# A hybrid encoder block on one core: query latent with its rows outermost, both halves of x in one 256-column block, norm scales per token

## The chip, the cores and the metric

One core of a Trainium2 chip runs one layer of a streaming encoder for 256 tokens. The metric is the device time of one execution in microseconds (us). PE is the matrix engine (TensorE), with a weight load (PEld) ahead of each matmul; DVE is VectorE, ACT is ScalarE, POOL is GpSimd, SP issues the transfers of weights.

## The reference, cut to what matters

```
u = rms_norm(x, norm_pre_mix)                      # x: 256 tokens x 2048
q_sb, k_sb, v_sb, q_lat, kv_lat, k_r, gates = split(u @ w_in)   # widths 1024, 1024, 1024, 768, 512, 64, 4096
y_sb  = stick_breaking_attention(q_sb, k_sb, v_sb) @ w_o_sb
q     = rms_norm(q_lat, q_norm) @ w_uq             # nope and rope parts of 8 heads
kv    = rms_norm(kv_lat, kv_norm) @ w_ukv
y_mla = mla_attention(q, rope(k_r), kv) @ w_o_mla
h     = x + rms_norm((gate_sb * y_sb + gate_mla * y_mla) @ w_out)
out   = h + rms_norm(swiglu(rms_norm(h)) @ w_down)
```

Everything is float32. `rms_norm(x, g)` divides each token by the root of its mean square and multiplies each column by g.

## The kernel before, in words

Every product of a weight w and an activation x is made of three fp32r products: both are split into a high part (an ACT copy to fp32r) and a low part (a DVE subtraction), and hi*hi + hi*lo + lo*hi is summed in PSUM. Weights stream from HBM in units of 128 x 1024 (512 KB) over SP's queue: `unit` (L88) issues the transfer into `raw`, ACT makes `hi` (L101), DVE makes `lo` (L102). There are four buffers of each.

The first stages put features on the output partitions and the 256 tokens on the columns. `pair` (L154) makes 256 features: for each row block k of 128 rows and each half j of 128 features it issues one matmul of 512 columns (the high weights times both halves of x, side by side, L164) and one of 256 columns (the low weights times the high half of x, L166). I call these two matmuls, for one k and one j, a step. The result lies in PSUM as two halves of 256 columns, which `fold` (L171) adds: an ACT copy of one half (L173), a DVE addition (L174), and where a norm scale applies a DVE multiplication by a row of 256 per-token scales (L176).

The order of the work: three pairs of the query latent (`lat_q`, 6 x 128 features), two of the key/value latent (`lat_kv`), the rope key (`kr`, the same two matmuls at L364 and L365), four pairs of `q_sb`, then from the latents `qn` (four pairs, K = 6 blocks), `qr` (two), `kn` (four, K = 4), then `vm`, `k_sb`, `v_sb` and the gates, and after them the output products and the SwiGLU. That is 536 steps: 96 for lat_q, 64 for lat_kv, 16 for kr, 128 each for q_sb and k_sb, 48 for qn, 24 for qr, 32 for kn. The later stages (`token` L178, `two_products` L612) use matmuls of 512 columns only.

The first pair also loads x: `load_first` (L212) puts the transfers of x (L113) between those of the weights, in small pieces for the first four row blocks, and ACT and DVE split x (L115, L116). So all 2 MB of x pass during the first pair, that is, during its four units.

The weights of the norms are folded into x or the latents; the per-token scales are applied after the products. `x_stats` (L227) sums squares of x (ACT squares, POOL additions), `x_scale` (L239) turns the sum over features into a row of scales (`row_sums`, L130, one fp32 matmul of 256 columns with ones) and into a column of scales (`col_sums`, L135), each through `rsqrt` (L120: ACT Sqrt and five DVE operations). `lat_scale` (L408) does the same for both latents. `angles` (L275) is a chain of DVE operations for the rope.

These side jobs are hung on unit numbers: `at_unit(u, f)` emits f behind the matmuls of unit u, and behind that unit's splits on ACT and DVE. The lat_q units are 0 to 11, lat_kv 12 to 19, kr 20 and 21, q_sb 22 to 37. Within these rules the framework's planner orders each engine's instructions; each engine then runs them in that order.

Of the kernel before, what the change touches and what calls it, by code (L numbers as in the profile page):

```python
# [53 lines left out]
def block_kernel(ctx: ExitStack, tc: tile.TileContext, a: dict, out: bass.AP):  # L54
# [14 lines left out]
    def at_bank(name):  # L69
        return pat.tile([P, 512], F32, tag="at", name=name)  # L70
# [17 lines left out]
    def unit(stream, cols_n, cuts=1, first=None):  # L88
        off = streams.get(stream, 0)
        streams[stream] = off + P * cols_n  # L90
        src = a[stream][off:off + P * cols_n].rearrange("(p c) -> p c", p=P)
        raw = wp.tile([P, 1024], F32, tag="raw", name=f"raw_{stream}_{off}", bufs=4)
        hi = wp.tile([P, 1024], F32R, tag="hi", name=f"hi_{stream}_{off}", bufs=4)
        lo = wp.tile([P, 1024], F32R, tag="lo", name=f"lo_{stream}_{off}", bufs=4)
        w = cols_n // cuts
        for c in range(cuts):
            cs = slice(c * w, c * w + w)
            if first:
                first(c)
# [30 lines left out]
    def row_sums(acc, name):  # L130
        ps = at_bank(f"{name}_row")
        TE.matmul(ps[:, :T], lhsT=ones, rhs=acc, start=True, stop=True)
        return ps[:, :T]
# [20 lines left out]
    def pair(name, stream, K, per, rhs, first=None):  # L154
        ps = mm_pair(f"{name}_ps")
        for u in range(K // per):
            cuts = (4 if u == 0 else 2) if first else 1
            hi, lo = unit(stream, per * 2 * P, cuts, first and (lambda c: first(u, c)))
            for i in range(per):
                k = u * per + i  # L160
                for j in range(2):
                    o = (i * 2 + j) * P
                    r = rhs(k)
                    TE.matmul(ps[:, j, :], lhsT=hi[:, o:o + P], rhs=r, start=k == 0, stop=False,  # L164
                              skip_group_check=True)
                    mm = TE.matmul(ps[:, j, 0:T], lhsT=lo[:, o:o + P], rhs=r[:, 0], start=False, stop=k == K - 1,  # L166
                                   skip_group_check=True)
            unit_done(mm)
        return ps

    def fold(ps, row, out_t):  # L171
        tb = tmp.tile([P, 2, T], F32, tag="t2", name="tb", bufs=6)
        S.activation(tb, ps[:, :, T:], AF.Copy)  # L173
        V.tensor_tensor(out_t, ps[:, :, 0:T], tb, op=ALU.add)  # L174
        if row is not None:
            V.tensor_tensor(out_t, out_t, row[:, None, :].to_broadcast([P, 2, T]), op=ALU.mult)  # L176
# [62 lines left out]
    def x_scale():  # L239
        acc = acc_x[0]  # L240
        v = slot("vx")[:, 0]
        V.tensor_scalar(v, row_sums(acc, "x"), 1.0 / D, EPS, op0=ALU.mult, op1=ALU.add)
        rsqrt(r0, v)
        vc = const.tile([P, 2], F32, tag="vxc", name="vxc")
        V.tensor_scalar(vc, col_sums(acc, "x"), 1.0 / D, EPS, op0=ALU.mult, op1=ALU.add)
        rsqrt(r0c, vc)
        V.tensor_tensor(r0_sq[:, 0], r0, r0, op=ALU.mult)
        V.tensor_tensor(r0c_sq, r0c, r0c, op=ALU.mult)
        V.tensor_scalar_mul(r0q, r0, SB_SCALE)
# [75 lines left out]
    lat = {}  # L325
    for nm, n in (("q", 6), ("kv", 4)):
        acc = slot(f"acc_{nm}")[:, 0]
        g = cols[f"{nm}_norm"]
        for p in range(n // 2):
            first = nm == "q" and p == 0  # L330
            ps = pair(f"lat_{nm}{p}", "w_lat", KD, 4, xk, load_first if first else None)
            s = tmp.tile([P, 2, T], F32, tag="t2", name="s", bufs=6)
            fold(ps, None, s)
# [14 lines left out]
        lat[nm] = acc  # L348

# [10 lines left out]
    for u in range(2):  # L360
        hi, lo = unit("w_kr", 1024)
        for i in range(8):
            k = u * 8 + i
            TE.matmul(kps, lhsT=hi[:, i * P:i * P + P], rhs=xs[:, k], start=k == 0, stop=False, skip_group_check=True)  # L364
            mm = TE.matmul(kps[:, 0:T], lhsT=lo[:, i * P:i * P + P], rhs=xs[:, k, 0], start=False, stop=k == KD - 1,  # L365
                           skip_group_check=True)
        unit_done(mm)
    kraw = slot("kraw")[:, 0]

    def take_k():  # L370
        kb = slot("kb")[:, 0]
        S.activation(kb, kps[:, T:], AF.Copy)
        V.tensor_tensor(kraw, kps[:, 0:T], kb, op=ALU.add)
        V.tensor_tensor(kraw, kraw, r0, op=ALU.mult)

    at_unit(count[0] + 1, take_k)
# [3 lines left out]
    def proj_q(p):  # L380
        ps = pair(f"q_sb{p}", "w_q", KD, 4, xk)
        t = slot(f"q_sb{p}")
        fold(ps, r0q, t)
        qsb.append(t)

    def proj_k(p):
        ps = pair(f"k_sb{p}", "w_k", KD, 4, xk)
        t = slot(f"k_sb{p}")
        fold(ps, r0, t)
        ksb.append(t)  # L390
# [12 lines left out]
    at_unit(26, rope_k)  # L403
# [446 lines left out]
def _lay_out(x, positions, norm_pre_mix, w_in, b_gate, q_norm, w_uq, kv_norm, w_ukv, w_o_sb, w_o_mla, w_out,  # L850
# [21 lines left out]
        "w_lat": _feature_units(w, 3072 + ar(1280), 4),  # L872
# [36 lines left out]
```

## Time and profile before

| what | us |
|---|---|
| median of 3 runs | 1394.98 (1394.79 to 1395.91) |
| the profiled execution | 1395.33 |
| its span, first to last instruction | 1393.6 |
| PE busy | 1373.6 |
| DVE busy | 804.1 |
| ACT busy | 681.1 |

Read the engines' busy shares first, then what PE waited for, then the stretch in which it waited.

### The profile page before, as it was taken

Reading aid. Unit: us, or ns where it says so; the run is one execution under the profiler, and the core shown is the slowest. Engines: PE = TensorE matmul, PEld = TensorE weight load, DVE = VectorE, ACT = ScalarE, POOL = GpSimd, SP = SyncE. Lnnn points to the kernel's source line nnn. Section 1 sums busy time; section 2 is a strip of 40 time slices with the busy share of each in tenths; the row PEclk is TensorE's granted clock in tenths of the full one; section 3 lists DMA queues with packets and bytes.
Section 4 is the critical chain, followed back from the end, with each engine's and each line's share of the span. In section 5 each row is a group of like instructions: output and inputs, shape, how many; then the busy total and the mean of one; then the engine's idle time right before and its main releaser. Section 6 shows DMA issues by size and latency. Waiting matters only on the chain.

```text
span 1393.6 us, 16788 instructions
## 1 busy us (share of the span) xinstructions
PE 1373.6 (99%) x6400; PEld 1141.1 (82%) x6400; DVE 804.1 (58%) x927; ACT 681.1 (49%) x816; POOL 59.2 (4%) x89
## 2 busy tenths in 40 slices
PE   7999999999999999999999999999999999999997
PEld 6888888888888888887888888888888888888886
DVE  7997966555555566557555545555455555444444
ACT  7564454466548443445644444444444454434343
POOL 3210000000002100000000000000000001000001
PEclk9999999999999999999999999999999999999999
DMA  7565655455567766664766666665656666666663
GB/s 239 186 207 164 199 167 166 153 182 183 172 209 250 219 184 190 185 196 121 218 190 184 192 186 193 184 191 185 195 185 192 184 207 205 192 196 195 195 188 116
DMA packets 74977, 262.88 MB, mean 189 GB/s; under 512 B 8592, under 2 KB 9744, under 8 KB 74768
## 3 DMA queue, kind: packets, MB, share of 16 engines
q1 hardware_dynamic: 72720, 254.86, 58.8%
q0 software_dynamic: 1744, 6.29, 1.4%
q8 instruction: 50, 0.82, 0.2%
q10 hardware_dynamic: 432, 0.66, 0.1%
q14 instruction: 31, 0.25, 0.0%
HBM read 259.68 MB, written 2.10 MB: 188 GB/s over the span
## 4 chain that ended last, share of the span: by engine, by line
PE 94%; DVE 3%; DMA 1%; ACT 1%; issue 1%; SPq 0%; POOL 0%; DVEq 0%; ACTq 0%
PE gu_ps L629 11%; PE gu_ps L631 11%; PE gu_ps L630 11%; PE wd_ps L200 6%; PE wd_ps L202 6%; PE wd_ps L201 6%; PE gate_ps L202 4%; PE gate_ps L200 4%; PE gate_ps L201 4%; PE k_sb_ps L164 2%; PE q_sb_ps L164 2%; PE wout_ps L200 2%; PE wout_ps L202 2%; PE wo_ps L631 2%; PE wo_ps L630 2%; PE wo_ps L629 2%
## 5 line engine op out<-in xcount | busy, mean ns | idle before, releaser
L773 DVE SCALAR_TENSOR_TENSOR lo_w_gu<-raw_w_gu,packed,hi_w_gu 128x1024 fp32r<-128x1024 f32 x172 | 221.0, 1285 | 213.3 <-ACT hi_w_gu L772 211.6
L772 ACT ACTIVATE hi_w_gu<-raw_w_gu,packed 128x1024 fp32r<-128x1024 f32 x172 | 198.0, 1152 | 230.4 <-PE gu_ps L630 226.4
L629 PE MATMUL gu_ps<-hi_w_gu,hs 128*128 128x512 f32 x704 | 276.6, 393 | 0.9 <-ACT hi_w_gu L766 0.9
L631 PE MATMUL gu_ps<-lo_w_gu,hs 128*128 128x512 f32 x704 | 275.1, 391 | 0.7 <-DVE lo_w_gu L767 0.7
L630 PE MATMUL gu_ps<-hi_w_gu,hs 128*128 128x512 f32 x704 | 273.5, 389 | 0.0
L102 DVE TENSOR_TENSOR lo_w_down<-raw_w_down,hi_w_down 128x1024 fp32r<-128x1024 f32 x88 | 109.2, 1242 | 120.4 <-ACT hi_w_down L101 120.1
L101 ACT ACTIVATE hi_w_down<-raw_w_down 128x1024 fp32r<-128x1024 f32 x88 | 93.3, 1061 | 135.6 <-PE wd_ps L201 127.4
L629 PEld LDWEIGHTS gu_ps<-hi_w_gu,hs 128*128 128x128 f32 x704 | 132.2, 188 | 31.2 <-ACT hi_w_gu L766 2.3
L631 PEld LDWEIGHTS gu_ps<-lo_w_gu,hs 128*128 128x128 f32 x704 | 132.1, 188 | 28.7 <-DVE lo_w_gu L767 1.4
L630 PEld LDWEIGHTS gu_ps<-hi_w_gu,hs 128*128 128x128 f32 x704 | 132.2, 188 | 27.1
L102 DVE TENSOR_TENSOR lo_w_gate<-raw_w_gate,hi_w_gate 128x1024 fp32r<-128x1024 f32 x64 | 78.7, 1234 | 70.1 <-ACT hi_w_gate L101 63.8
L200 PE MATMUL gate_ps<-hi_w_gate,xs 128*128 128x512 f32 x256 | 100.6, 393 | 0.0
L202 PE MATMUL gate_ps<-lo_w_gate,xs 128*128 128x512 f32 x256 | 99.7, 390 | 0.0
L201 PE MATMUL gate_ps<-hi_w_gate,xs 128*128 128x512 f32 x256 | 99.6, 389 | 0.0
L101 ACT ACTIVATE hi_w_gate<-raw_w_gate 128x1024 fp32r<-128x1024 f32 x64 | 67.4, 1055 | 62.0 <-PE gate_ps L201 53.7
L102 DVE TENSOR_TENSOR lo_w_out<-raw_w_out,hi_w_out 128x1024 fp32r<-128x1024 f32 x32 | 39.2, 1226 | 38.8 <-ACT hi_w_out L101 38.6
L101 ACT ACTIVATE hi_w_o<-raw_w_o 128x1024 fp32r<-128x1024 f32 x32 | 34.0, 1061 | 51.7 <-PE wo_ps L630 45.2
L102 DVE TENSOR_TENSOR lo_w_o<-raw_w_o,hi_w_o 128x1024 fp32r<-128x1024 f32 x32 | 39.2, 1225 | 32.0 <-ACT hi_w_o L101 31.4
L101 ACT ACTIVATE hi_w_out<-raw_w_out 128x1024 fp32r<-128x1024 f32 x32 | 34.0, 1061 | 47.2 <-PE wout_ps L201 36.3
L202 PEld LDWEIGHTS gate_ps<-lo_w_gate,xs 128*128 128x128 f32 x256 | 48.0, 188 | 10.1
L201 PEld LDWEIGHTS gate_ps<-hi_w_gate,xs 128*128 128x128 f32 x256 | 48.1, 188 | 9.7
L200 PEld LDWEIGHTS gate_ps<-hi_w_gate,xs 128*128 128x128 f32 x256 | 48.1, 188 | 9.6
(447 smaller groups left out, 2557.0 us busy)
## 6 DMA issues: line engine op xcount, KB each, us to landing
raw_w_gu<-in_w_gu SPq DMA_DIRECT2D x176, 512.0 KB, 3.6
raw_w_down<-in_w_down SPq DMA_DIRECT2D x88, 512.0 KB, 3.5
raw_w_gate<-in_w_gate SPq DMA_DIRECT2D x64, 512.0 KB, 3.6
raw_w_o<-in_w_o SPq DMA_DIRECT2D x32, 512.0 KB, 3.8
raw_w_out<-in_w_out SPq DMA_DIRECT2D x32, 512.0 KB, 3.5
raw_w_lat<-in_w_lat SPq DMA_DIRECT2D x16, 512.0 KB, 4.8
raw_w_q<-in_w_q SPq DMA_DIRECT2D x16, 512.0 KB, 4.0
raw_w_k<-in_w_k SPq DMA_DIRECT2D x16, 512.0 KB, 3.8
```

Of the source, the lines that this page charges most:

```text
L101: split_ins[0] = S.activation(hi[:, cs], raw[:, cs], AF.Copy)
L102: split_ins[1] = V.tensor_tensor(lo[:, cs], raw[:, cs], hi[:, cs].bitcast(F32), op=ALU.subtract)
L164: TE.matmul(ps[:, j, :], lhsT=hi[:, o:o + P], rhs=r, start=k == 0, stop=False, skip_group_check=True)
L200: TE.matmul(ps[t], lhsT=l[0][:, ts], rhs=hi[:, cs], start=k == 0, stop=False)
L201: TE.matmul(ps[t], lhsT=l[1][:, ts], rhs=hi[:, cs], start=False, stop=False)
L202: mm = TE.matmul(ps[t], lhsT=l[0][:, ts], rhs=lo[:, cs], start=False, stop=k == K - 1)
L629: TE.matmul(ps[t][:, j], lhsT=x[0][:, ts], rhs=hi[j], start=k == 0, stop=False)
L630: TE.matmul(ps[t][:, j], lhsT=x[1][:, ts], rhs=hi[j], start=False, stop=False)
L631: mm = TE.matmul(ps[t][:, j], lhsT=x[0][:, ts], rhs=lo[j], start=False, stop=k == K - 1)
L772: split_ins[0] = S.activation(hi, raw, AF.Copy, scale=g)
L773: split_ins[1] = V.scalar_tensor_tensor(lo, raw, g, hi.bitcast(F32), op0=ALU.mult, op1=ALU.subtract)
```

## The change

The query latent is no longer three pairs one after the other. `first_products` runs over the 16 row blocks k outermost: one unit is now 128 rows x 768 features (384 KB), and for each k all six feature blocks are multiplied, into three PSUM banks that stay open together; the last two row blocks go bank by bank, so that the banks end one after the other. `load_x` is called as the row blocks come. A step is now `block`: three matmuls of 256 columns into one 256-column block (hi times x hi, hi times x lo, lo times x hi), in `pair`, in `first_products` and for `kr`. A pair then needs one bank, and there are no halves to add: `scaled` is one DVE multiplication that reads PSUM, and the latents are read by ACT and DVE straight from PSUM. The norm scales are worked out for [128, 2] columns only (`col_sums`, `rsqrt` on two columns); `spread` makes rows of them: for each 128 tokens a DVE multiplication of a block of ones by the column, a matmul with the identity (fp32, 128 columns), and an ACT copy with a factor. The side jobs hang on other unit numbers (q latent 0 to 15, kv latent 16 to 23, kr 24 and 25, q_sb 26 to 41). The host lays out the q part of `w_lat` in row order.

```diff
-    def row_sums(acc, name):
-        ps = at_bank(f"{name}_row")
-        TE.matmul(ps[:, :T], lhsT=ones, rhs=acc, start=True, stop=True)
+    def spread(col, name, *rows):
+        ps = at_bank(f"{name}_row")
+        b = tmp.tile([P, 2, P], F32, tag="t2", name="b", bufs=6)
+        for t in range(2):
+            V.tensor_scalar_mul(b[:, t], ones, col[:, t:t + 1])
+            TE.matmul(ps[:, t * P:t * P + P], lhsT=b[:, t], rhs=ident, start=t == 0, stop=True, skip_group_check=True)
+        for row, factor in rows:
+            S.activation(row, ps[:, :T], AF.Copy, scale=factor)
...
+    def block(ps, hi, lo, x, start, stop):
+        TE.matmul(ps, lhsT=hi, rhs=x[:, 0], start=start, stop=False, skip_group_check=True)
+        TE.matmul(ps, lhsT=hi, rhs=x[:, 1], start=False, stop=False, skip_group_check=True)
+        return TE.matmul(ps, lhsT=lo, rhs=x[:, 0], start=False, stop=stop, skip_group_check=True)
...
-                    TE.matmul(ps[:, j, :], lhsT=hi[:, o:o + P], rhs=r, start=k == 0, stop=False,
-                              skip_group_check=True)
-                    mm = TE.matmul(ps[:, j, 0:T], lhsT=lo[:, o:o + P], rhs=r[:, 0], start=False, stop=k == K - 1,
-                                   skip_group_check=True)
+                    mm = block(ps[:, j], hi[:, o:o + P], lo[:, o:o + P], rhs(k), k == 0 and j == 0, k == K - 1)
...
-    def fold(ps, row, out_t):
-        tb = tmp.tile([P, 2, T], F32, tag="t2", name="tb", bufs=6)
-        S.activation(tb, ps[:, :, T:], AF.Copy)
-        V.tensor_tensor(out_t, ps[:, :, 0:T], tb, op=ALU.add)
-        if row is not None:
-            V.tensor_tensor(out_t, out_t, row[:, None, :].to_broadcast([P, 2, T]), op=ALU.mult)
+    def scaled(ps, row, out_t):
+        V.tensor_tensor(out_t, ps, row[:, None, :].to_broadcast([P, 2, T]), op=ALU.mult)
...
-    for u in range(3, 12):
+    for u in [*range(2, 17, 2), 17]:
         at_unit(u, lambda: next(stat_steps, None))
     at_unit(8, constants)
-    at_unit(18, x_scale)
-    for u in [*range(5, 14), 16]:
+    at_unit(22, x_scale)
+    at_unit(24, lambda: spread(r0c, "r0", (r0, 1.0), (r0q, SB_SCALE)))
+    for u in (17, 19, 21, 23, 25, 27, 29, 31, 33, 35):
         at_unit(u, lambda: next(trig_steps, None))
...
+    def first_products():
+        both = mm_pair("lat_q_ps")
+        ps = [x.rearrange("p (j t) -> p j t", j=2) for x in (both[:, 0], both[:, 1], at_bank("lat_q2_ps"))]
+        order = [(k, p) for k in range(KD - 2) for p in range(3)]
+        order += [(k, p) for p in range(3) for k in range(KD - 2, KD)]
+        w = {}
+        for k, p in order:
+            if k not in w:
+                if k < 4:
+                    load_x(k, 1)
+                elif k % 2 == 0:
+                    load_x(k, 2)
+                w[k] = unit("w_lat", 768, 3 if k < 2 else 1)
+            hi, lo = w[k]
+            for j in range(2):
+                o = (2 * p + j) * P
+                mm = block(ps[p][:, j], hi[:, o:o + P], lo[:, o:o + P], xk(k), k == 0 and j == 0, k == KD - 1)
+            if p == 2:
+                unit_done(mm)
+            if k == KD - 1:
+                yield ps[p]
...
-    at_unit(count[0] + 1, take_k)
+        V.tensor_tensor(kraw, kps[:, 0:T], r0, op=ALU.mult)
+    at_unit(count[0] + 2, take_k)
...
-    at_unit(25, lambda: lat_scale(rq, row_sums, lat["q"], r0, r0_sq[:, 0], 768, "q", MLA_SCALE))
-    at_unit(29, lambda: lat_scale(rkv, row_sums, lat["kv"], r0, r0_sq[:, 0], 512, "kv"))
-    at_unit(32, lambda: lat_scale(rkvc, col_sums, lat["kv"], r0c, r0c_sq, 512, "kvc"))
+    at_unit(27, lambda: lat_scale(rqc, "q", 768))
+    at_unit(28, lambda: lat_scale(rkvc, "kv", 512))
+    at_unit(30, lambda: spread(rqc, "rq", (rq, MLA_SCALE)))
+    at_unit(31, lambda: spread(rkvc, "rkv", (rkv, 1.0)))
```

## Rows read from the trace of the kernel before

**Rows 1.** The page's first part: busy time, share of the span, instructions.

```profile
PE 1373.6 (99%) x6400; PEld 1141.1 (82%) x6400; DVE 804.1 (58%) x927; ACT 681.1 (49%) x816; POOL 59.2 (4%) x89
```

**Rows 2.** Waits of PE, whole span: total us, times, longest us.

```profile
PE lat_q_ps L164 <- DVE xs L116: 4.7, 1, 4.7
PE lat_q_ps L166 <- DVE lo_w_lat L102: 2.6, 5, 1.0
PE lat_q_ps L164 <- ACT hi_w_lat L101: 1.2, 1, 1.2
...
PE lat_kv_ps L166 <- DVE lo_w_lat L102: 0.4, 1, 0.4
```

**Rows 3.** Busy per window: length, PE, PEld, DVE, ACT, POOL, clock, DMA share, GB/s.

```profile
10.00:20.00 10.00, 8.39 (x43) 6.37 (x43) 8.43 (x18) 8.43 (x18) 0.00 (x0) 1.00 1.00 367
...
4.60:10.60 6.00, 5.83 (x16) 4.32 (x16) 3.80 (x9) 3.56 (x8) 0.00 (x0) 1.00 0.83 234
```

**Rows 4.** Timeline of PE, the query latent: start us, length us, instruction.

```profile
4.69 0.77 PE L164 MATMUL lat_q_ps<-xs,hi_w_lat 128*128 128x512 f32 x1 [4.69 <-DVE xs L116]
...
6.11 0.63 PE L164 MATMUL lat_q_ps<-xs,hi_w_lat 128*128 128x512 f32 x1
...
6.75 0.63 PE L164 MATMUL lat_q_ps<-xs,hi_w_lat 128*128 128x512 f32 x1
...
11.68 0.50 PE L164 MATMUL lat_q_ps<-xs,hi_w_lat 128*128 128x512 f32 x1 [1.16 <-ACT hi_w_lat L101]
...
33.27 0.39 PE L164 MATMUL lat_q_ps<-xs,hi_w_lat 128*128 128x512 f32 x1
...
46.70 0.40 PE L164 MATMUL lat_kv_ps<-xs,hi_w_lat 128*128 128x512 f32 x1
```

**Rows 5.** Timeline of PE around the stick-breaking sums, 298 to 301 us.

```profile
298.64 0.39 PE L201 MATMUL gate_ps<-hi_w_gate,xs 128*128 128x512 f32 x1
...
299.77 0.40 PE L546 MATMUL z<-sphl,negT_r 128*128 128x256 f32 x2
300.01 0.40 PE L548 MATMUL z<-sph,negT_r 128*128 128x512 f32 x1
...
300.48 0.39 PE L550 MATMUL z<-sphl,negones_r 128*128 128x256 f32 x2
300.70 0.40 PE L200 MATMUL gate_ps<-hi_w_gate,xs 128*128 128x512 f32 x1
```

**Rows 6.** Timeline of PEld, the weight loads, in the same place.

```profile
299.89 0.19 PEld L548 LDWEIGHTS z<-sph,negT_r 128*128 128x128 f32 x1
```

**Rows 7.** Tiles q_sb_ps and qn_ps on PE: min/median/max ns, first and last start.

```profile
L164 PE MATMUL q_sb_ps<-xs,hi_w_q x128: 391/395/586, 76.5 to 122.5; 128*128 128x512 f32 x128
...
L164 PE MATMUL qn_ps<-lat_q,hi_w_uqn x48: 392/394/395, 122.8 to 139.1; 128*128 128x512 f32 x48
```

**Rows 8.** Chain that ended last, in order of time: start us, us, what.

```profile
87.93 0.43 PE q_row L132 x2
```

**Rows 9.** Timeline of ACT in the first pair; brackets: idle before, released by.

```profile
8.37 0.42 ACT L101 ACTIVATE hi_w_lat<-raw_w_lat 128x256 fp32r<-128x256 f32 x1 [0.83 <-DMA raw_w_lat<-in_w_lat]
...
10.99 0.63 ACT L101 ACTIVATE hi_w_lat<-raw_w_lat 128x512 fp32r<-128x512 f32 x1 [1.02 <-DMA raw_w_lat<-in_w_lat]
```

**Rows 10.** Groups by line and shape, 0 to 172 us: count, busy us, mean ns.

```profile
L102 DVE TENSOR_TENSOR lo_w_uqn<-raw_w_uqn,hi_w_uqn 128x768 fp32r<-128x768 f32 x8 | 7.7, 957 | 7.4 <-ACT hi_w_uqn L101 7.4
...
L116 DVE SCALAR_TENSOR_TENSOR xs<-xT,packed,xs 128x256 fp32r<-128x256 f32 x16 | 7.2, 483 | 4.5 <-ACT xs L115 4.4
...
L101 ACT ACTIVATE hi_w_uqn<-raw_w_uqn 128x768 fp32r<-128x768 f32 x8 | 6.8, 847 | 10.9 <-PE q_sb_ps L164 5.7 <-PE qn_ps L164 4.0 <-issue 1.2
...
L233 POOL TENSOR_TENSOR ssx<-ssx,sq 128x512 f32<-128x512 f32 x7 | 10.5, 1500 | 0.4
```

**Rows 11.** Timeline of DVE, the column scale of x, first and last operation.

```profile
73.94 0.15 DVE L245 TENSOR_SCALAR vxc<-x_col 128x2 f32<-128x2 f32 x1
...
82.73 0.15 DVE L248 TENSOR_TENSOR r0c_sq<-r0c 128x2 f32<-128x2 f32 x1
```

More of the change, by code (lines that the diff above doesn't have):

```diff
@@ L86, in block_kernel, with unit @@
     streams, split_ins = {}, [None, None]
-    def unit(stream, cols_n, cuts=1, first=None):
+    def unit(stream, cols_n, cuts=1):
         off = streams.get(stream, 0)
@@ L152, in unit_done, with pair @@
                 fn()
-    def pair(name, stream, K, per, rhs, first=None):
-        ps = mm_pair(f"{name}_ps")
+    def block(ps, hi, lo, x, start, stop):
+        TE.matmul(ps, lhsT=hi, rhs=x[:, 0], start=start, stop=False, skip_group_check=True)
+        TE.matmul(ps, lhsT=hi, rhs=x[:, 1], start=False, stop=False, skip_group_check=True)
+        return TE.matmul(ps, lhsT=lo, rhs=x[:, 0], start=False, stop=stop, skip_group_check=True)
+    def pair(name, stream, K, per, rhs):
+        ps = mm_pair(f"{name}_ps")[:, 0].rearrange("p (j t) -> p j t", j=2)
         for u in range(K // per):
-            cuts = (4 if u == 0 else 2) if first else 1
-            hi, lo = unit(stream, per * 2 * P, cuts, first and (lambda c: first(u, c)))
+            hi, lo = unit(stream, per * 2 * P)
             for i in range(per):
@@ L239, in x_scale @@
     def x_scale():
[L240 to L243, printed above, removed]
         vc = const.tile([P, 2], F32, tag="vxc", name="vxc")
-        V.tensor_scalar(vc, col_sums(acc, "x"), 1.0 / D, EPS, op0=ALU.mult, op1=ALU.add)
+        V.tensor_scalar(vc, col_sums(acc_x[0], "x"), 1.0 / D, EPS, op0=ALU.mult, op1=ALU.add)
         rsqrt(r0c, vc)
-        V.tensor_tensor(r0_sq[:, 0], r0, r0, op=ALU.mult)
         V.tensor_tensor(r0c_sq, r0c, r0c, op=ALU.mult)
-        V.tensor_scalar_mul(r0q, r0, SB_SCALE)
     ident = const.tile([P, P], F32, tag="ident", name="ident")
@@ L329, in block_kernel @@
         for p in range(n // 2):
[L330 to L333, printed above, removed]
+            s = next(q_products) if nm == "q" else pair(f"lat_{nm}{p}", "w_lat", KD, 4, xk)
             sq = tmp.tile([P, 2, T], F32, tag="t2", name="sq", bufs=6)
@@ L348, in block_kernel @@
         lat[nm] = acc
+    next(q_products, None)
     def rope_of(raw, name):
@@ L363, in block_kernel @@
             k = u * 8 + i
-            TE.matmul(kps, lhsT=hi[:, i * P:i * P + P], rhs=xs[:, k], start=k == 0, stop=False, skip_group_check=True)
-            mm = TE.matmul(kps[:, 0:T], lhsT=lo[:, i * P:i * P + P], rhs=xs[:, k, 0], start=False, stop=k == KD - 1,
-                           skip_group_check=True)
+            mm = block(kps[:, 0:T], hi[:, i * P:i * P + P], lo[:, i * P:i * P + P], xs[:, k], k == 0, k == KD - 1)
         unit_done(mm)
@@ L382, in proj_q @@
         t = slot(f"q_sb{p}")
-        fold(ps, r0q, t)
+        scaled(ps, r0q, t)
         qsb.append(t)
@@ L388, in proj_k @@
         t = slot(f"k_sb{p}")
-        fold(ps, r0, t)
+        scaled(ps, r0, t)
         ksb.append(t)
@@ L401, in rope_k @@
         V.tensor_tensor(krr, u1, u2, op=ALU.add)
-    at_unit(26, rope_k)
+    at_unit(38, rope_k)
     rlat = slot("rlat")
@@ L406, in block_kernel, with lat_scale @@
     rkvc = const.tile([P, 2], F32, tag="rkvc", name="rkvc")
-    def lat_scale(r, sums, acc, r_x, r_x_sq, n, name, scale=None):
-        v = slot(f"v_{name}").rearrange("p a b -> p (a b)")[:, :r.free_size()]
-        V.scalar_tensor_tensor(v, sums(acc, name), 1.0 / n, r_x_sq, op0=ALU.mult, op1=ALU.mult)
+    rqc = const.tile([P, 2], F32, tag="rqc", name="rqc")
+    def lat_scale(r, nm, n):
+        v = const.tile([P, 2], F32, tag=f"v_{nm}", name=f"v_{nm}")
+        V.scalar_tensor_tensor(v, col_sums(lat[nm], nm), 1.0 / n, r0c_sq, op0=ALU.mult, op1=ALU.mult)
         V.tensor_scalar_add(v, v, EPS)
         rsqrt(r, v)
-        V.tensor_tensor(r, r, r_x, op=ALU.mult)
-        if scale:
-            V.tensor_scalar_mul(r, r, scale)
-    at_unit(25, lambda: lat_scale(rq, row_sums, lat["q"], r0, r0_sq[:, 0], 768, "q", MLA_SCALE))
-    at_unit(29, lambda: lat_scale(rkv, row_sums, lat["kv"], r0, r0_sq[:, 0], 512, "kv"))
-    at_unit(32, lambda: lat_scale(rkvc, col_sums, lat["kv"], r0c, r0c_sq, 512, "kvc"))
+        V.tensor_tensor(r, r, r0c, op=ALU.mult)
+    at_unit(27, lambda: lat_scale(rqc, "q", 768))
+    at_unit(28, lambda: lat_scale(rkvc, "kv", 512))
+    at_unit(30, lambda: spread(rqc, "rq", (rq, MLA_SCALE)))
+    at_unit(31, lambda: spread(rkvc, "rkv", (rkv, 1.0)))
     for p in range(4):
@@ L426, in block_kernel @@
         t = slot(f"qn{p}")
-        fold(ps, rq, t)
+        scaled(ps, rq, t)
         qn.append(t)
@@ L449, in block_kernel @@
         t = slot(f"kn{p}")
-        fold(ps, rkv, t)
+        scaled(ps, rkv, t)
         kn.append(t)
```

21 lines of the change are left out of this document (5 added, 16 removed).

## The prediction

> **What bounds the kernel now.** I read the busy shares first: PE is busy for 1373.6 of 1393.6 us [rows 1], so the kernel is one long row of matmuls, and DVE and ACT matter only where PE waits for them. So the second view is PE's waits. Nearly all stand in the query latent: 4.7 us before the first matmul, 2.6 us for low weights, 1.2 us for high weights [rows 2]. The third view is the timeline of that stretch, because the wait rows don't hold what a slow matmul costs. It runs from 4.69 to 46.70 us [rows 4]: 42.0 us for 96 steps. A step late in it takes 0.353 us: 38 steps lie between the starts at 33.27 and 46.70. 96 of these are 33.9 us, so 8.1 us are lost there, and two things lose them. The first steps take 0.64 us (6.11 to 6.75): 768 columns at 1.2 per ns, the lower of TensorE's two levels, though the clock column reads 1.00 in that window [rows 3]; PE had done nothing before 4.69, had worked nearly without a break until 10.5, and the matmul after the gap, at 11.68, is already shorter. Eight such steps lose some 2.3 us. The rest, 5.8 us, is waiting for data: all of x (2 MB) and 2 MB of weights must come while PE does only 32 of its steps, some 11 us of work, and between 10 and 20 us the DMA engines are full (share 1.00, 367 GB/s) [rows 3].
>
> The span lies 1.7 us below the profiled execution's own 1395.33, which is 0.35 above the median. I make the sum on the span and take it off the median.
>
> **Part 1: rows outermost in the query latent.** Now x comes over the whole latent: per row block 128 KB of x and 384 KB of weights (0.52 MB) for six steps, 2.1 us. At 367 GB/s that is 1.4 us, so transfers get ahead of PE where they fell behind it. I walk through the start. The first matmul stays near 4.7: its two transfers keep their places at the head of SP's queue. SP issues more transfers at first (three cuts of the first two units), but of the same 128 KB as before. Twelve steps belong to the first two row blocks; at 0.64 until about 10.9 (the middle of the change of level seen in rows 4) PE does 9.7 of them, the other 2.3 take 0.8: 11.7 us. The eighth 128 KB piece is in at 8.37 and 1.5 MB at 10.99 [rows 9]; in the new order 1.5 MB is where the third unit's weights are whole. Its split costs ACT 0.85 and DVE 0.96 [rows 10], so its low weights are there at 12.8: PE waits about 1.1 us, and ends this row block at 14.7. The next unit (0.5 MB more, 1.4 us) lands at 12.4 and is split by 14.2, in time. From there 13 row blocks of six steps at 0.346 us (part 2) take 27.0: end at 41.7. DVE needs 0.96 + 0.48 a row block [rows 10], under 2.08; POOL's additions of squares (1.5 us each, seven) now fall in this stretch and I take 0.3 us of late splits for them, between nothing and 1.5. So the latent ends at 42.0 instead of 46.7: **-4.7 us**, between -5.8 (no wait at the third unit) and -3.2 (POOL's worst). At its end the ACT queue holds three latent banks to be read. The two buffers of row blocks 12 and 13 are free by then and cover the first two units of lat_kv; without that cover PE would wait about 2.6 us once.
>
> **Part 2: a step is three matmuls of 256 columns.** The columns stay 768; there are 536 more matmuls and weight loads. The trace has no long run of such matmuls, but pairs: the two of L546 take 0.24 us together (299.77 to 300.01), the two of L550 0.22 (300.48 to 300.70), so 0.115 each and 0.346 for three [rows 5]. The load that comes with each is not in the way: the one for the matmul at 300.01 begins at 299.89 and its record lasts 0.19 us [rows 6], so a matmul can start 0.12 us after its load has begun. Steps of today: qn 47 steps in 16.3 us, 0.347; q_sb 127 steps in 46.0 us [rows 7], less three fp32 products of 0.43 [rows 8] and a column sum that lie among them, 0.351. I count 0.351 for lat_kv, kr, q_sb, k_sb and kn (368 steps) and 0.347 for qn and qr (72): 368 x 0.005 + 72 x 0.001 = **-1.9 us**. The bounds: 512 columns alone take 0.226 (five from 298.64 to 299.77), and at that rate a step is 0.339, -5.0 us; at the longest single spacing that rounding allows (0.119) it is 0.357, +2.9. I take the middle, which is what the rows show.
>
> **Part 3: no halves to add.** In 18 pairs an ACT copy and a DVE addition go, and in the five latent pairs too. I count nothing: PE's own work hides them, and would have to be short for this to show. What it can give is the small waits in which DVE was late: 0.4 us at lat_kv [rows 2] and a little around kn. **-0.6 us**, between 0 and -1. DVE is nearest to full there, so this relief is also the cover for part 1's POOL term.
>
> **Part 4: scales per token.** Three row sums of 256 fp32 columns go, three spreads of 2 x 128 columns come: the same columns. New are the query latent's column sums, four passes of one column; between 0 and four spacings of 0.115: 0.46; I take 0.15, since one column is nearer to nothing. DVE's wide rsqrt operations go, narrow ones of 0.15 us come [rows 11]. New is a wait: the spread's matmul stands in PE's order behind a DVE product that needs the whole column chain. All later matmuls queue behind it. I take 0.3 us for the three. Together **+0.45 us**.
>
> Sum: -4.7 - 1.9 - 0.6 + 0.45 = -6.75 us. After 172 us nothing is touched and PE stays full, so the gain is not given back: 1394.98 - 6.75 = **1388.2 us**.
>
> **The rivals.**
>
> A. PE waits at the spreads. x_scale hangs on unit 22, its spread on unit 24: two units of eight steps, 5.5 us. Before, the chain from the first to the last column operation took 8.8 us (73.94 to 82.73) [rows 11]. If the new one took as long, PE would stand 3.3 us instead of 0.3: 1391.2. For it: DVE runs in order and is crowded there. Against it: the row operations that lay between are gone, and the other two spreads have three units each.
>
> B. A matmul has a fixed cost. If the 0.013 us by which a 512-column matmul exceeds 512 columns at 2.4 GHz (0.226 against 0.213) is paid per matmul, a 256-column one takes 0.120, a step 0.360: the 78 fast steps of lat_q lose 1.1, the others 368 x 0.009 + 72 x 0.013 = 4.2 instead of winning 1.9. The sum is +0.5: 1395.4, no change. Against it: pairs at 0.11 to 0.12 [rows 5]. Beside it stands the Trainium skill, TensorE: Matmul & The Clock Gate, "Wait — 56ns, not 53.3ns?": a matmul's start-to-start time is its columns at 2.4 GHz and a fixed 2.5 ns. By that page each added matmul costs 2.5 ns, 440 of them +1.1 us in place of part 2's -1.9, and the time, an estimate by the page, would be 1391.2; the trace agrees only in part, since its 512-column spacing is 226 ns and not the page's 215.7.
>
> C. Slower: the weight load binds. In a run of 256-column matmuls each load has only one of them to hide under. If the load's whole 0.19 us record [rows 6] had to pass between two starts, a step would take 0.56, 518 x 0.218 = 113 us more: 1501. The point from which it decides is low: at 0.1198 us a matmul the whole gain is gone, above 0.1216 the change is slower by over 0.2%. Against it: the matmul at 300.01, which started 0.12 us after its load [rows 5, 6].
>
> D. The start stays bound by transfers. If they kept to the rate between 8.37 and 10.99, 0.5 MB in 2.6 us [rows 9], each row block would take 2.6 us instead of 2.08, lat_q would end near 46.7, and -2.05 remains: 1392.9. Against it: the full rate in the window from 10 us on.
>
> **How the numbers follow.** Forecast 0.70, A 0.12, B 0.08, C 0.05, D 0.05. The forecast's own terms reach from about 1384 to 1391; A lies at the upper end, and the range goes on to 1392.5, which leaves out B, C, D and the tails. Faster by over 0.2% (2.8 us, about what a measurement of this kernel can tell from no change) are the forecast and A: 0.82; within 0.2% B and D: 0.13; slower C: 0.05.
>
> **What would show it.** lat_q's last matmul near 42 us, with one wait near 12; if it ends past 45 with DMA full, D. Steps of 0.34 to 0.35 us in q_sb and kn; 0.36 is B, more is C. No idle PE before the spreads' matmuls with the identity; a wait of some 3 us behind unit 23 is A. From 172 us on, everything as before but earlier by the same amount. I would be wrong if the pace of three 256-column matmuls differs from that of pairs, or if ACT reads the latent banks ahead of lat_kv's first weights.

## The result: 1399.0 us, slower by 4.1, and the profile after

| what | before | after |
|---|---|---|
| median of 8 runs each, us | 1394.93 (1393.87 to 1395.91) | 1399.02 (1398.66 to 1401.39) |
| ratio, 95% interval | | 1.0031 (1.0022 to 1.0040) |
| the profiled execution | 1395.33 | 1401.39 |
| its span | 1393.6 | 1399.7 |

The forecast was 1388.2, in a range from 1384.0 to 1392.5: wrong in sign and outside its range. The profiled execution of after is the longest of its eight, 2.4 us above the median; its trace holds a stretch at the lower clock early in the latent that the experiments' traces don't have, so I take the size of the whole change from the medians, and only mechanisms and the size of single waits from the trace.

The first part of the page of after answers to [rows 1]:

```profile
PE 1379.2 (99%) x6946; PEld 1173.9 (84%) x6946; DVE 776.8 (55%) x894; ACT 668.7 (48%) x795; POOL 62.9 (4%) x89
```

DVE and ACT have 27 and 12 us less to do, as the change says; PE has 546 more matmuls and 5.6 us more of busy time, though the columns are nearly the same. PE's waits in the whole span (total us, times, longest), which answer to [rows 2]:

```profile
PE lat_q_ps L159 <- ACT hi_w_lat L99: 6.1, 2, 4.4
PE r_row L141 <- DVE b L140: 3.4, 1, 3.4
PE gu_ps L640 <- DVE lo_w_gu L776: 0.7, 2, 0.4
PE gu_ps L638 <- ACT hi_w_gu L775: 0.7, 1, 0.7
PE lat_q_ps L161 <- DVE lo_w_lat L100: 0.5, 1, 0.5
```

The query latent's waits behind its first matmul have shrunk from 3.8 to some 2.2 us, and the second line is new: 3.4 us at the spread of x's scale. The timeline of PE there (start, length, instruction, idle time before it and its releaser):

```profile
71.95 0.28 PE L160 MATMUL kr_ps<-xs,hi_w_kr 128*128 128x256 f32 x1
75.62 1.02 PE L141 MATMUL r_row<-ident,b 128*128 128x128 f32 x4 [3.39 <-DVE b L140]
76.30 0.56 PE L161 MATMUL kr_ps<-xs,lo_w_kr 128*128 128x256 f32 x1
76.66 0.41 PE L159 MATMUL kr_ps<-xs,hi_w_kr 128*128 128x256 f32 x1
76.87 0.41 PE L160 MATMUL kr_ps<-xs,hi_w_kr 128*128 128x256 f32 x1
...
79.22 0.32 PE L159 MATMUL kr_ps<-xs,hi_w_kr 128*128 128x256 f32 x1
79.37 0.28 PE L160 MATMUL kr_ps<-xs,hi_w_kr 128*128 128x256 f32 x1
```

In the middle of the rope key's matmuls PE stands still until 75.62, and then it works slowly: the starts from 76.66 to 79.22 lie 0.213 us apart, where 0.120 is usual in this kernel. 256 columns in 0.213 us are 1.2 per ns, the lower of the two levels. Busy time by window says the same (length, PE, PEld, DVE, ACT, POOL, granted clock, DMA share, GB/s):

```profile
72.00:75.60 3.60, 0.23 (x2) 0.03 (x1) 3.60 (x13) 0.78 (x2) 2.52 (x8) 1.00 0.40 107
75.60:79.60 4.00, 3.98 (x20) 3.98 (x21) 3.77 (x10) 0.66 (x2) 0.00 (x0) 0.57 0.64 210
```

From 75.62 to 79.37 PE did a spread (0.45 us at full pace in a later run) and 14 matmuls at 0.12: 2.1 us of work in 3.75. So the lower clock cost 1.6 us on top of the wait, about 5 us together. DVE is busy for the whole of the first window: PE waits for an engine that is full. What DVE does there, from the column sum's first operation to the block of ones:

```profile
67.85 0.15 DVE L235 TENSOR_SCALAR vxc<-x_col 128x2 f32<-128x2 f32 x1
...
68.77 1.22 DVE L100 TENSOR_TENSOR lo_w_q<-raw_w_q,hi_w_q 128x1024 fp32r<-128x1024 f32 x1
...
72.59 0.43 DVE L288 TENSOR_TENSOR turn<-turn,pr 128x256 f32<-128x256 f32 x1
72.93 0.15 DVE L126 TENSOR_TENSOR r0c<-r0c,newton 128x2 f32<-128x2 f32 x1
73.00 1.22 DVE L100 TENSOR_TENSOR lo_w_q<-raw_w_q,hi_w_q 128x1024 fp32r<-128x1024 f32 x1
...
75.30 0.47 DVE L140 TENSOR_SCALAR b<-ones,r0c 128x128 f32<-128x128 f32 x2
```

The scale column is ready at 73.1, yet the block of ones comes at 75.30: between them lie a split of q's weights, two steps of `angles` and a piece of the key/value latent. The chain takes 7.5 us from 67.85 to 75.30, though most of its own operations take 0.15 us.

The second change shows in the tile rows (min/median/max ns, first and last start), which answer to [rows 7]:

```profile
L159 PE MATMUL q_sb_ps<-xs,hi_w_q x128: 280/283/469, 79.6 to 127.5; 128*128 128x256 f32 x128
L159 PE MATMUL qn_ps<-lat_q,hi_w_uqn x48: 283/283/283, 127.9 to 144.8; 128*128 128x256 f32 x48
L159 PE MATMUL kr_ps<-xs,hi_w_kr x16: 283/283/415, 68.2 to 79.2; 128*128 128x256 f32 x16
```

qn makes 47 steps in 16.9 us, 0.360 a step; before it was 0.347. And kr begins at 68.2 us; before it was 70.8, by this row of the trace of before:

```profile
L364 PE MATMUL kr_ps<-xs,hi_w_kr x16: 389/398/403, 70.8 to 76.1; 128*128 128x512 f32 x16
```

So 2.6 us of part 1's gain are there even in this execution.

### The profile page after: what moved, and what is told of

Its sections match the earlier page's. It is cut to its first block, busy times and chain, and to the rows that moved or that the text cites. A ratio compares the mean times of both kernels' runs of the same rounds, so it can differ in the third digit from the quotient of the medians.

```text
span 1399.7 us, 17831 instructions
## 1 busy us (share of the span) xinstructions
PE 1379.2 (99%) x6946; PEld 1173.9 (84%) x6946; DVE 776.8 (55%) x894; ACT 668.7 (48%) x795; POOL 62.9 (4%) x89
## 4 chain that ended last, share of the span: by engine, by line
PE 96%; DVE 2%; DMA 0%; ACT 0%; SPq 0%; issue 0%; POOL 0%; DVEq 0%; ACTq 0%
PE gu_ps L640 11%; PE gu_ps L638 11%; PE gu_ps L639 11%; PE wd_ps L200 6%; PE wd_ps L201 6%; PE wd_ps L202 6%; PE gate_ps L200 4%; PE gate_ps L202 4%; PE gate_ps L201 4%; PE wout_ps L200 2%; PE wo_ps L640 2%; PE wout_ps L202 2%; PE wo_ps L638 2%; PE wo_ps L639 2%; PE wout_ps L201 2%; PE q_sb_ps L159 1%
## 5 line engine op out<-in xcount | busy, mean ns | idle before, releaser
L202 PEld LDWEIGHTS gate_ps<-lo_w_gate,xs 128*128 128x128 f32 x256 | 48.0, 188 | 10.3
```

What stands on the lines that cost most here:

```text
L202: mm = TE.matmul(ps[t], lhsT=l[0][:, ts], rhs=lo[:, cs], start=False, stop=k == K - 1)
```

## The experiments

Edits are against the changed kernel unless said otherwise; "before" is the kernel before on the same chip, with a median between 1394.7 and 1395.0 each time (e1 to e4 ran on one chip, e5 to e8 on another, e9 and e10 on a third). There were three theories. T1: the wait at the spread, with the lower clock after it, is what turned the sign. T2: a step of three 256-column matmuls is slower than one of two. T3: rows outermost doesn't bring what I forecast.

**e1: the spread of x's scale three units later.** All else stays.

```diff
-    at_unit(24, lambda: spread(r0c, "r0", (r0, 1.0), (r0q, SB_SCALE)))
+    at_unit(27, lambda: spread(r0c, "r0", (r0, 1.0), (r0q, SB_SCALE)))
```

> The changed kernel with one number changed: the spread that makes the row r0 hangs on unit 27 instead of unit 24. Theory: PE's wait of 3.4 us for the spread's DVE product is a plain loss, and the clock's fall behind it (12 steps or so at half speed, 1.7 us) comes from that wait. Both should go: 3.4 to 5.4 us less than the changed kernel, so about 1394 to 1395.5, beside the kernel before or a little under it. No idle PE between 70 and 80 us, no matmul of 0.21 us spacing there. Rival: the wait is only pushed on, since DVE is late with its whole queue; then a wait of 2 us or more stands at the new place or at the first use of the row, and the time stays at 1398 to 1399.

Measured: 1393.81 (1393.44 to 1394.22), ratio 0.9990 (0.9981 to 0.9999), 5.2 us less than after. The first row is the tile kr, the second the window from 70 to 80 us, both of this run:

```profile
L159 PE MATMUL kr_ps<-xs,hi_w_kr x16: 283/283/283, 66.0 to 71.4; 128*128 128x256 f32 x16
...
70.00:80.00 10.00, 10.00 (x87) 10.00 (x86) 9.86 (x26) 4.18 (x7) 2.32 (x8) 1.00 0.50 147
```

No idle time, clock 1.00, and DVE is as full as it was (9.86 of 10 us): the wait came from where the consumer stood in PE's order, not from the amount of work. The 3.4 of the wait and the 1.6 at the lower clock make up 5.0 of the 5.2 us. And kr begins 4.8 us earlier than before (66.0 against 70.8).

**e9: the spread stays, the angle steps move.** The other way to make the chain short.

```diff
-    for u in (17, 19, 21, 23, 25, 27, 29, 31, 33, 35):
+    for u in (27, 28, 29, 30, 31, 32, 33, 34, 35, 36):
         at_unit(u, lambda: next(trig_steps, None))
```

> The changed kernel with the rope angles' DVE steps moved from units 17, 19, ... to units 27 to 36; the spread of r0 stays on unit 24, the steps stay three matmuls of 256 columns. It asks why the spread is late. Theory: DVE runs in order, and between the narrow operations of the column chain the planner has put angle steps and weight splits; without the angles the chain takes 4 us or less instead of 7.5, PE waits at most 1 us at the spread and the clock doesn't fall: 1394 to 1395.5. Rival: the chain is long by itself (eight short operations with a Sqrt on ACT between, each behind a weight split of 1.2 us); then the wait stays above 2 us and the time above 1396.5.

Measured: 1394.23, ratio 0.9996 (0.9986 to 1.0005), with no wait at the spread and no lower clock. DVE's chain in this run:

```profile
63.41 0.16 DVE L235 TENSOR_SCALAR vxc<-x_col 128x2 f32<-128x2 f32 x1 [0.97 <-PE x_col L131]
...
66.02 0.16 DVE L126 TENSOR_TENSOR r0c<-r0c,newton 128x2 f32<-128x2 f32 x1
...
66.29 0.48 DVE L140 TENSOR_SCALAR b<-ones,r0c 128x128 f32<-128x128 f32 x2
```

2.9 us from first to last start instead of 7.5, and DVE has idle time again. The chain was long because DVE had angle steps in its order between the chain's links. That is shown: nothing else was moved.

**e2: the old step everywhere but in lat_q, the spread stays at unit 24.**

```diff
-                    mm = block(ps[:, j], hi[:, o:o + P], lo[:, o:o + P], rhs(k), k == 0 and j == 0, k == K - 1)
+                    mm = wide(ps[:, j], hi[:, o:o + P], lo[:, o:o + P], rhs(k), k == 0, k == K - 1)
...
+    def wide(ps, hi, lo, x, start, stop):
+        TE.matmul(ps, lhsT=hi, rhs=x, start=start, stop=False, skip_group_check=True)
+        return TE.matmul(ps[:, 0:T], lhsT=lo, rhs=x[:, 0], start=False, stop=stop, skip_group_check=True)
```

With it the old `fold` comes back in these stages.

> The changed kernel with the old step in lat_kv, kr, q_sb, k_sb, qn, qr and kn: one matmul of 512 columns and one of 256, the two halves added by an ACT copy and a DVE addition. The query latent keeps its 256-column steps and its rows outermost, and the scales stay per token. Theory: a matmul costs 0.0133 us beside its columns, so a step goes from 0.360 back to 0.347 to 0.351, 440 steps: 4 to 4.5 us less than the changed kernel, about 1394.5 to 1395, with the wait at the spread still there. Rival: the step's pace is set by something else (for instance by the state of the clock), and steps of 0.36 are no slower in sum; then the time stays within 1 us of the changed kernel's 1399.

Measured: 1393.47, ratio 0.9991 (0.9981 to 1.0001), 5.5 us less than after. The wait did not stay the same size, as this row of PE's waits and the window from 70 to 74 us show:

```profile
PE r_row L141 <- DVE b L140: 1.7, 1, 1.7
...
70.00:74.00 4.00, 4.00 (x24) 3.53 (x25) 4.00 (x9) 3.17 (x7) 3.27 (x7) 1.00 0.02 6
```

The wait is half as long, the clock stays at 1.00 behind it, and both count into the 5.5 us. So e2 alone gives no size for the step.

**e3: e1 and e2 together.**

> Both edits at once: the spread of r0 on unit 27 and the old two-matmul step everywhere but in the query latent. Theory: the two losses are apart from each other and add up, 7.5 to 9.5 us less than the changed kernel: 1389.5 to 1391.5, under the kernel before by 3.5 to 5.5 us. Rival: with the halves to be added again, DVE and ACT are too full for the column chain, and a wait comes back: no better than 1394.

Measured: 1393.39, ratio 0.9989 (0.9980 to 0.9999). A miss: the two edits are not additive. With the late spread and the full DVE work of `fold`, PE waits at the next spread, hung on unit 30:

```profile
PE rq_row L141 <- DVE b L140: 1.0, 1, 1.0
PE rq_row L141 <- DVE rkvc L126: 1.0, 1, 1.0
```

It looks like the same mechanism one place further on, so the comparison needed all three spreads out of the way.

**e5 and e10: all spreads late, old step against new step.** e10 is the changed kernel with the three spreads moved; e5 has in addition e2's `wide` and `fold`.

```diff
-    at_unit(24, lambda: spread(r0c, "r0", (r0, 1.0), (r0q, SB_SCALE)))
+    at_unit(27, lambda: spread(r0c, "r0", (r0, 1.0), (r0q, SB_SCALE)))
...
-    at_unit(30, lambda: spread(rqc, "rq", (rq, MLA_SCALE)))
-    at_unit(31, lambda: spread(rkvc, "rkv", (rkv, 1.0)))
+    at_unit(36, lambda: spread(rqc, "rq", (rq, MLA_SCALE)))
+    at_unit(37, lambda: spread(rkvc, "rkv", (rkv, 1.0)))
```

> As the kernel with the late spread and the old steps together, and the spreads of rq and rkv moved too, from units 30 and 31 to 36 and 37 (their rows are first read after unit 43 and later). That kernel showed PE waiting twice for about 1.05 us at rq's spread. Theory: these waits are the reason why the two edits did not add up; without them 2.1 us go: 1391 to 1391.5. No wait of PE between 12 us and the SwiGLU but the small ones of the kernel before. Rival: what was saved at r0 comes back in q_sb whatever the hooks, since DVE's work is the same; the time stays at 1393 to 1393.5.

> The changed kernel with all three spreads late (units 27, 36, 37) and all steps three matmuls of 256 columns: beside the kernel with all spreads late and the old steps (1391.2) it differs in the form of the step alone, with no wait of PE in either. Theory: 440 steps of 0.360 instead of 0.347 to 0.354: 2.5 to 4.4 us more than that one, 1393.7 to 1395.5. Rival: the addition of the halves on ACT and DVE costs the old form as much as the pace costs the new one, or the difference seen between the earlier kernels was in their waits: within 1 us of 1391.2.

Measured: e5 1391.15 (1390.42 to 1391.57), ratio 0.9971 (0.9959 to 0.9982); e10 1394.02, ratio 0.9994 (0.9985 to 1.0003). e5 is the fastest kernel of this study, 3.7 us under before. The two differ in the form of 440 steps and in the `fold` that belongs to the old form: 2.9 us in favour of the old one, or 3.2 by the two ratios, since the runs were on two chips. Tile rows of e5, then of e10:

```profile
L164 PE MATMUL kr_ps<-xs,hi_w_kr x16: 391/391/391, 66.4 to 71.6; 128*128 128x512 f32 x16
...
L164 PE MATMUL q_sb_ps<-xs,hi_w_q x128: 391/391/582, 72.0 to 119.0; 128*128 128x512 f32 x128
...
L164 PE MATMUL k_sb_ps<-xs,hi_w_k x128: 389/398/582, 169.1 to 248.5; 128*128 128x512 f32 x128
```

```profile
L159 PE MATMUL kr_ps<-xs,hi_w_kr x16: 283/283/283, 66.4 to 71.8; 128*128 128x256 f32 x16
...
L159 PE MATMUL q_sb_ps<-xs,hi_w_q x128: 280/283/469, 72.2 to 120.6; 128*128 128x256 f32 x128
...
L159 PE MATMUL k_sb_ps<-xs,hi_w_k x128: 277/283/469, 171.0 to 251.3; 128*128 128x256 f32 x128
```

With the same other work in it, q_sb takes 47.0 us in e5 and 48.4 in e10; k_sb begins 1.9 us later in e10, and its span is 2.8 us longer (1392.6 against 1389.8). Since both begin kr at 66.4, these 2.8 us come from the 376 steps behind that point. The 64 steps of lat_kv cost e10 some 0.5 us more as well, but its waits at the third unit of the query latent are 1.0 us shorter (0.7 against 1.7). Neither kernel waits at a spread.

**e4: the cost of a matmul by itself.** q_sb's steps are six matmuls of 128 columns; the product is the same.

```diff
+    def halved(ps, hi, lo, x, start, stop):
+        for l, h in ((hi, 0), (hi, 1), (lo, 0)):
+            for c in range(2):
+                cs = slice(c * P, c * P + P)
+                mm = TE.matmul(ps[:, cs], lhsT=l, rhs=x[:, h, cs], start=start and l is hi and h == 0 and c == 0,
+                               stop=stop and l is lo, skip_group_check=True)
...
-        ps = pair(f"q_sb{p}", "w_q", KD, 4, xk)
+        ps = pair(f"q_sb{p}", "w_q", KD, 4, xk, halved)
```

> The changed kernel with each matmul of the q_sb pairs cut in two of 128 columns: six matmuls and six weight loads a step instead of three, the same columns; all else as it is. It measures the disputed cost by itself. If a matmul has a fixed cost of 0.0133 us beside its columns at 2.4 GHz, one of 128 columns takes 0.067 us, a step 0.400 instead of 0.360, and q_sb (128 steps) gets 5.1 us longer. If instead the weight load sets the 0.120 us seen in the changed kernel, a matmul can't start less than 0.12 us after the one before, a step takes 0.72 and q_sb gets 46 us longer.

Measured: 1439.23 (one run), 40 us more than after, where the two theories gave 5 and 46: a miss for both. The tile row of q_sb's high-weight matmuls, and three records of PE's timeline in it:

```profile
L167 PE MATMUL q_sb_ps<-xs,hi_w_q x512: 272/276/410, 77.8 to 165.5; 128*128 128x128 f32 x171
...
99.77 0.39 PE L167 MATMUL q_sb_ps<-xs,hi_w_q 128*128 128x128 f32 x2
99.99 0.39 PE L167 MATMUL q_sb_ps<-xs,lo_w_q 128*128 128x128 f32 x2
100.22 0.61 PE L167 MATMUL q_sb_ps<-xs,hi_w_q 128*128 128x128 f32 x4
```

Four matmuls from 99.77 to 100.22: 0.112 us each, and q_sb takes 88 us where e10 takes 48. Half the columns save 0.008 us only. A pure fixed cost would have given 0.067, so there is a floor of 0.112 for such a matmul of 128 columns that brings its own weights. Beside it stands the Trainium skill, TensorE: Matmul & The Clock Gate, "LDWEIGHTS (loading the stationary operand)": a load takes its columns at 1.2 per ns, by that page an estimate of 107 ns for 128. The trace agrees within 6 ns if the load is the floor, which is an inference: no run here changes the load alone.

**e7: e5 with the old step in lat_q as well,** in six PSUM banks.

```diff
-        ps = [x.rearrange("p (j t) -> p j t", j=2) for x in (both[:, 0], both[:, 1], at_bank("lat_q2_ps"))]
+        other = mm_pair("lat_q1_ps")
+        ps = [[both[:, 0], both[:, 1]], [other[:, 0], other[:, 1]], [at_bank("lat_q2_ps"), at_bank("lat_q3_ps")]]
...
-                mm = block(ps[p][:, j], hi[:, o:o + P], lo[:, o:o + P], xk(k), k == 0 and j == 0, k == KD - 1)
+                mm = wide(ps[p][j], hi[:, o:o + P], lo[:, o:o + P], xk(k), k == 0, k == KD - 1)
```

> As the one with all spreads late, but the query latent too is made of the old steps, 512 and 256 columns, in six PSUM banks, with the halves added. So rows outermost and scales per token are left of the change, and nothing of the 256-column block. Theory: 96 steps by 0.009 us, 0.9 us less. Rival: with six banks taken the key/value latent has to wait for the first pair to be read, and ACT and DVE have the halves to add at the same place: a wait of 1 us or more at the end of the query latent eats it up.

Measured: 1391.36, ratio 0.9977 (0.9967 to 0.9987), the same as e5. Its profile reaches kr at 64.8 us, 1.6 before e5, but has the same span (1389.8). In the execution that was traced its lead over e5 is 1.6 us there, 0.9 at the last matmul of the down projection (1379.51 against 1380.43), and nothing at the end: the tail behind that matmul is 10.3 us instead of 9.4. Neither loss could be placed. Inconclusive.

**e6: e5 with the first four units in three cuts** (`3 if k < 4 else 1` in place of `3 if k < 2 else 1`), to take away the wait at the third unit.

> As the one with all spreads late, and the third and fourth unit of the query latent also come in three cuts of 256 columns. PE then can begin the third row block with its first 128 KB. Theory of the start: the wait of some 0.6 to 0.8 us at the third unit is that for a whole 384 KB transfer and its split; it shrinks to under 0.3: 0.3 to 0.6 us less than without the cuts. Rival: the bytes set it, the smaller transfers land no earlier in sum, and the four more transfer issues of 0.45 us on SP push later ones back: no gain, or up to 1 us more.

Measured: 1392.76, ratio 0.9986 (0.9977 to 0.9995), 1.6 us worse than e5. Another miss. Its profile reaches kr only 0.6 us earlier (65.8 against 66.4), since the wait moved on to x: PE's timeline has 1.1 us idle before the matmul at 16.93. Why the whole is longer stays open; the traced execution again has the longer tail, 10.5 us.

**e8: rows outermost alone.** This is the kernel before with `first_products` (old steps, six banks as in e7) and the unit numbers of the changed kernel for its side jobs: x's scale and the latents' scales four units later, but the angle steps 12 to 20 units later, and `rope_k` on unit 38 instead of 26. `row_sums`, `fold` and the wide operations on rows of scales stay as they were.

```diff
-    at_unit(18, x_scale)
+    at_unit(22, x_scale)
-    for u in [*range(5, 14), 16]:
+    for u in (17, 19, 21, 23, 25, 27, 29, 31, 33, 35):
         at_unit(u, lambda: next(trig_steps, None))
...
-    at_unit(25, lambda: lat_scale(rq, row_sums, lat["q"], r0, r0_sq[:, 0], 768, "q", MLA_SCALE))
+    at_unit(29, lambda: lat_scale(rq, row_sums, lat["q"], r0, r0_sq[:, 0], 768, "q", MLA_SCALE))
```

> The kernel before with the rows outermost in the query latent and nothing else of the change: old steps in six banks, row sums and wide scale rows as before, the side jobs moved on by the four units that the latent has more. Theory of the first part: the stretch to the end of lat_kv gets 4.7 to 5.5 us shorter and nothing later gives it back: 1389.5 to 1390.5. Rival: the wide scale rows, now 4 us nearer to their use, or the late rope angles, make PE wait in q_sb or at the ropes: 1392 or more.

Measured: 1397.72, ratio 1.0024 (1.0014 to 1.0033), slower than before, though kr begins at 65.7 us instead of 70.8. The largest row of PE's waits, then two records of DVE's timeline and two of PE's behind the wait:

```profile
PE q_sb_ps L166 <- DVE lo_w_q L102: 6.4, 1, 6.4
...
67.38 1.75 DVE L124 RECIPROCAL r<-r 128x256 f32<-128x256 f32 x1
...
76.89 1.22 DVE L102 TENSOR_TENSOR lo_w_q<-raw_w_q,hi_w_q 128x1024 fp32r<-128x1024 f32 x1
...
78.54 0.63 PE L164 MATMUL q_sb_ps<-xs,hi_w_q 128*128 128x512 f32 x1
...
79.18 0.63 PE L164 MATMUL q_sb_ps<-xs,hi_w_q 128*128 128x512 f32 x1
```

DVE works without a break from 66 to 78 us: the wide scale chain (one reciprocal is 1.75 us), angle steps and sums of halves stand ahead of the split of q's first weights. PE waits 6.4 us for it and goes on at 0.64 us a step until 81.10, where 0.35 is usual: four such steps and a slow one on either side, some 1.5 us more. So part 1 needs a DVE that is relieved in this place. From 66.30 to 76.89 us DVE spends 5.3 us on the scale of x, 3.9 on angle steps and 1.4 on the key/value latent. The angle steps did not stand here before, so e8 is not rows outermost alone, and no run has rows outermost with wide scales and early angles: how much of the 6.4 us the wide scales cost by themselves stays open. The narrow scales of part 4 relieve DVE, but they bring the spread's wait along; the gain is kept with the spread late (e1) or with the angle steps late (e9).

## Why the prediction was wrong

**The sum.** Of the parts as measured: part 1 -4.8 (kr's start in e1), the form of the step +2.9 (e10 less e5), the wait and the lower clock +5.2 (e1 less after), and 0.36 for the query latent's column sum (below). That makes +3.7 against 4.1 measured. Two corrections: the 2.9 and the 4.8 overlap by 0.6, since 64 steps of the key/value latent are in both; and some 0.4 of the 4.8 only moved, since the row sum of x lay ahead of kr (67.2 us in the trace of before) and the spread that replaces it lies behind kr's start. That gives +3.5, so 0.6 us stays unplaced; the interval of the ratio is 1.3 us to either side. Without the wait the change gives -1.1 us (e1): the wait and the clock behind it turned the sign. Without the new step as well it gives -3.7 (e5), still short of the -6.75 forecast.

**Part 1 was right in size, though its path varied.** Forecast -4.7, measured -4.8 in e1 and -4.4 in e5 and e10 at kr's start; in e1 and e10 the 64 slower steps of lat_kv stand before that point. The third unit's data came about when I said: its first matmul with low weights starts at 12.0 us in e1, 12.8 in e10 and 13.3 in e5 (forecast 12.8). What lies before that did not go as I walked through it: the upper clock came at 9.0 to 10.3 us in these three and at 7.6 in after, not at 10.9, and PE waits at this unit for 0.3 us in e1, 0.7 in e10 and 1.7 in e5 (1.2 for high weights, 0.5 for low; forecast 1.1). That the size fits so well is partly luck, since the 78 fast steps also lost 1.1 us to part 2's error. What I had not seen is that the planner lets the first unit of lat_kv start before the query latent ends (41.0 against 43.5 us in e1). In e7 and e8 it does not, and lat_kv still follows without a wait. Rival D did not come.

**Part 2 failed by its reading of [rows 5].** I put 0.115 us on a matmul of 256 columns from two pairs, and did not look at what stands beside them. The rows between the pairs, also from the trace of before:

```profile
300.01 0.40 PE L548 MATMUL z<-sph,negT_r 128*128 128x512 f32 x1
300.24 0.40 PE L548 MATMUL z<-spl,negT_r 128*128 128x512 f32 x1
300.48 0.39 PE L550 MATMUL z<-sphl,negones_r 128*128 128x256 f32 x2
```

Two matmuls of 512 columns take 0.47 us there, 0.235 each, where a long run of them has 0.227 (46 spacings from 289.10 to 299.55 in the same trace). What the 256s seemed to save, their neighbours paid: a start-to-start time belongs to two matmuls of different lengths. Closed over the whole group, from 299.77 to 300.70, it is 0.93 us; less two at 0.227 leaves 0.476 for four, 0.119 each. Nor was my 0.119 a bound on what rounding allows: the pair of L546 by itself reads 0.24 us, 0.120 each. The long runs of after have 0.120 (three records of PE's timeline, 0.36 us for one step):

```profile
99.74 0.28 PE L159 MATMUL q_sb_ps<-xs,hi_w_q 128*128 128x256 f32 x1
99.86 0.28 PE L160 MATMUL q_sb_ps<-xs,hi_w_q 128*128 128x256 f32 x1
...
100.10 0.28 PE L159 MATMUL q_sb_ps<-xs,hi_w_q 128*128 128x256 f32 x1
```

So rival B came, which I had given 0.08: a step is 0.360. Of its price, 4.2 us for the 440 steps outside lat_q, 2.9 came by the medians. The traces place most of the rest: for the 376 steps from kr on B's rates give 3.7 us, and e10 loses 2.8. Some 0.5 is missing in qn and qr, where e5's old step takes 0.353 us (47 in 16.6 us; before 0.347), and some 0.5 in kn and vm, where e5 gains nothing. Why the old step has two paces stays open. Rival C named the point where the gain is gone, 0.1198 us a matmul, and the real value stands on it. A floor of the kind that C feared shows in e4, but only below 256 columns: 0.112 is under 0.120.

**Part 4 failed by its price for the wait.** I put 0.3 us on three spreads and priced the alternative, rival A, at 3.3 us from the 8.8-us chain of [rows 11]. The wait was 3.4 us and the chain 7.5. The rows were right and the choice between them wrong: I took the row operations that are gone as relief, and did not list what the new unit numbers put in their place. The diff moves the angle steps to units 17 to 35, on both sides of the spread; e9 shows that they were the crowd. That A's 3.3 comes so near to 3.4 is partly luck: the chain was 1.3 us shorter than A had it, but it also began late, 2.6 us behind the end of the column sum that it reads (65.28 to 67.85 us in after). And A's price left out the lower clock, 1.6 us. Besides, the column sum of the query latent takes 0.36 us and not 0.15: in e10 its four passes run from 78.42 to 78.78, where the next matmul starts:

```profile
78.42 0.50 PE L131 MATMUL q_col<-ones,acc_q 128*128 128x1 f32 x4
```

The trace of before had such a sum (the tile kvc_col, 108.49 to 108.85), which I did not look up.

**Part 3** can't be told apart: `fold` and the old step come and go together in e2, e5 and e10, and 2.9 us is the sum of both. The wait of 0.4 us at lat_kv is gone in after, but also in e5, which has the folds, so the -0.6 us of this part are not shown. Once the spreads were late, only e7 has a PE wait that names a fold, 0.2 us at vm.

**The chances.** I treated A and B as exclusive, each against the rest of the forecast. They are independent parts of one kernel, and both came: the forecast of 1388.2 with A's 3.0, B's 7.2 and the 1.6 of the lower clock gives 1400.0. That this lies so near to 1399.0 is partly luck, since B's price did not come in full.

## What to carry to other kernels

Take the cost of a short instruction from a group that is closed on both sides by the same kind of neighbour, not from the gap that follows it. Where the critical engine's next instruction needs a result of another engine, write out all that the emission order puts between the links of that result's chain, and hang the consumer behind it; in e1 a consumer three units later cost nothing. Price a wait on TensorE together with the clock after it, and add up rivals that sit in different parts instead of choosing one.

## What the runs showed of the hardware

A matmul with its own weight load, back to back: 0.227 us for 512 columns, 0.120 for 256, 0.112 for 128. The first two differ by the 0.107 us that 256 columns take at 2.4 per ns and so share some 0.013 us beside their columns; the third stands on a floor. Beside it stands the Trainium skill, TensorE: Matmul & The Clock Gate, "Wait — 56ns, not 53.3ns?", which gives 2.5 ns for that share; here the trace does not agree, and the measurement decides.

TensorE's granted clock fell to the lower level behind an idle stretch of 3.4 us (after) and of 6.4 us (e8) and took 1.6 and 1.5 us; behind 1.7 us (e2) it did not. In the profiled execution of after it fell once more, without any long wait:

```profile
12.10:20.00 7.90, 7.41 (x47) 7.20 (x48) 7.56 (x10) 6.64 (x13) 2.97 (x2) 0.78 0.89 307
```

Ahead of it PE had been idle for 1.6 us and then for 0.5 more, close together, and its clock had risen early, at 7.6 us. The traces of e10 (0.2 and 0.5 us in the same place) and e5 (1.2 and 0.5) kept their clock. This fall, which cost some 1.5 us, is seen in one execution only; which of these differences brought it about no run here shows.
